# An ordering pass that counts a longer time for each transfer and lets at most eight be in flight

## The chip, the cores and the metric

The kernel runs on one core of a Trainium2 chip. The metric is the device time of one execution in microseconds (us). Three runs of the kernel before gave 2766.01, 2767.27 and 2772.61 us; the median is 2767.27 us. A profile is one more execution, recorded by the hardware profiler.

## The reference

The input x has 2048 tokens of 1024 numbers, in float32. One layer is computed:

```python
xn = rms_norm(x, mix_norm_g)
aq, ak, av, mq, mk, mv, mo, i, f, ga, gm = split(xn @ w_in)
att = chunk_band_attention(aq, ak, av, rel_bias)      # 8 heads of 64, own chunk of 64 + 8 before it
q, k = silu(causal_conv(mq, mk))                      # 4 taps
hm = rms_norm(mlstm_chunkwise(q, k, mv, i, f))        # 4 heads of 128, carried state per chunk
y = sigmoid(ga) * (att @ w_att_proj) + sigmoid(gm) * (sigmoid(mo) * hm @ w_mlstm_proj)
x = x + y @ w_out
x = x + square(relu(rms_norm(x) @ w_up)) @ w_down     # 1024 -> 4096 -> 1024
out = rms_norm(x)
```

All products must be good to float32.

## The kernel before, in words

**The work.** The tokens are cut into four blocks of 512. A product of float32 operands is made from three matmuls on rounded halves: each operand is split into a high part, rounded to the engine's fast float format, and the rest. For a weight tile ACT makes the high part (L611) and DVE the rest (L613, both in `split_now`); for an activation tile the same is done at L1321 and L1326 (`split`). The matmuls stand in `mm3` (L694 to L696) for plain products, at L779 (`quad`) and L808 (`quad_tok`) for products that are cut into seven instead of eight sub-products, with sums and differences of operands and results made by DVE (L1964 and others) and ACT (L1956 and others).

**The tiles.** On-chip tiles have fixed names and numbers of buffers: 4 `wraw` (a raw weight tile, 512 KB), 3 `wsp` (a split one), 28 `r` (split activations, 512 columns, two parts), 16 `ctx`, 6 `tmp`, 8 `bank` (PSUM). What does not fit is kept in HBM under names such as `qfar`, `kfar`, `vspill` (attention operands), `mfar`, `mvfar` (mLSTM operands), `u` (the hidden part of the feed-forward), `wsum` (differences of weight tiles). Weight loads are issued at L575, stores of all kinds at L2217 (`store`), loads of u and of mixed results at L2279 (`take_u1`), attention loads at L1350 (vspill), L1371 (kfar) and L1375 (qfar), mLSTM loads at L1715 and L1828. All of them but one small load go through the queue of the SyncE engine (SP). Transfers share eight semaphores, in turn.

At L1170 to L1175 (`norm_in`) a block of x is loaded, squared by ACT (L1172) and summed by DVE (L1175). At L1543 to L1548 (`turn`) attention probabilities are transposed by PE and split by ACT and DVE. L1512 is a matmul of scores, L1485 of probabilities with values; L1772 and L1797 are matmuls of the mLSTM part, fed by mfar and mvfar.

**The order.** It is made in two steps, both on the host, both when the program is built. First the class `Flow` runs the whole kernel as cooperating threads with estimated durations and so fixes the order in which instructions are written, and which buffer each uses. Then the class `Order` (L226) takes the finished list and orders it anew for each engine:

- `cost` and `transfer` give an estimated duration for each instruction and each transfer; `graph` finds who must wait for whom, from the regions that are read and written.
- `due` goes backwards: PE's instructions get the times at which they would run one after the other without a pause, and every other instruction the latest time at which it may start so that none of its users is late. A transfer is taken at 365 ns of SP plus `FAR`, 2500 ns, there.
- `run` (L338) goes forwards, as a simulation. It picks the engine that is free first, gives it the ripe instruction (one whose inputs are there by the estimates) with the earliest due time, PE alone the next in program order, and moves that engine's clock. A transfer costs SP 365 ns; it then passes one common queue, one after another, `REACH` (1400 ns) after the issue, for as long as `transfer` says, and has landed `LAND` (1100 ns) later. Users of what it brings become ripe on another engine only with a margin more (`MARGIN`, 2500 ns behind a transfer).
- The orders found are written into the program as fixed sequences. The pass leaves no times in it: on the chip an engine takes its instructions in that order, each as soon as its semaphores allow.

The functions that the change touches, and what calls them:

Of the kernel before, what the change touches and what calls it, by code (L numbers as in the profile page):

```python
# [96 lines left out]
class Flow:  # L97
# [77 lines left out]
    def run(self):  # L175
        while self.ready or self.blocked:
            moved = True
            while moved:
                moved = False
                for th in sorted(self.blocked, key=lambda x: (x.prio, x.n)):  # L180
                    ok, value = self._grant(th)
                    if ok:
                        self.blocked.remove(th)
                        self.now = th.at
                        self._step(th, value)
                        moved = True
            if not self.ready and not self.blocked:
                break
            if not self.ready:
                raise RuntimeError("no thread can go on")  # L190
            best = None
            for th in self.ready:
                t, frm = th.at
                for e in th.req[0].split("|"):
                    prio = th.prio
                    if e[-1] == "!":
                        e, prio = e[:-1], -1
                    start = t + self.LAT[frm].get(e, 0.0)
                    if e == "pe" and th.prio < 5:
                        start += self.SLACK  # L200
                    key = (max(self.clock[e], start), prio, th.n)
                    if best is None or key < best[0]:
                        best = (key, th, e)
            (start, _, _), th, e = best
            self.ready.remove(th)
            end = start + th.req[1]
            self.clock[e] = end
            if len(th.req) > 2:
                end += th.req[2]
            th.at = self.now = (end, e)  # L210
            self._step(th, e)
# [14 lines left out]
class Order:  # L226
# [1 line left out]

    MARGIN = dict(PE=600.0, Activation=100.0, DVE=100.0, Pool=100.0, SP=2500.0)
    WAKE = dict(PE=43.0, DVE=23.0, Activation=23.0, Pool=69.0, SP=16.0)  # L230
    REACH, LAND, FAR = 1400.0, 1100.0, 2500.0

    def __init__(self, tc):
        self.tc = tc
# [50 lines left out]
    def transfer(self, i):  # L285
        a, b = self.operands((i.outs[0], i.ins[0]))
        rows = min(list(x.ap)[0][1] for x in (a, b))
        t = self.count(a) * list(a.ap)[0][1] * 0.0099
        return max(60.0, t * (1.45 if 32 < rows <= 64 else 1.0))

    def graph(self):
# [46 lines left out]
    def run(self):  # L338
        due, n = self.due(), len(self.ins)
        at, safe, left = [0.0] * n, [0.0] * n, self.left  # L340
        clock = dict.fromkeys(self.WAKE, 0.0)
        soon = {e: [] for e in self.WAKE}
        ripe = {e: [] for e in self.WAKE}
        order = {e: [] for e in self.WAKE}
        queue = 0.0
        for k in range(n):
            if not left[k]:
                heapq.heappush(soon[self.eng[k]], (0.0, due[k], k))
        for _ in range(n):
            t, e = min((clock[e] if ripe[e] else max(clock[e], soon[e][0][0]), e)  # L350
                       for e in self.WAKE if ripe[e] or soon[e])
            while soon[e] and soon[e][0][0] <= t:
                k = heapq.heappop(soon[e])[2]
                heapq.heappush(ripe[e], (k if e == "PE" else due[k], k))
            k = heapq.heappop(ripe[e])[1]
            order[e].append(self.ins[k])
            start = max(clock[e], at[k])
            clock[e] = end = start + self.dur[k]
            if e == "SP":
                queue = max(queue, start + self.REACH) + self.transfer(self.ins[k])  # L360
                end = queue + self.LAND
            for j in self.succ[k]:
                to = self.eng[j]
                r = end + self.lag(k, j)
                at[j] = max(at[j], r)
                safe[j] = max(safe[j], r + (self.MARGIN[e] if to != "PE" and (to != e or e == "SP") else 0.0))
                left[j] -= 1
                if not left[j]:
                    heapq.heappush(soon[to], (safe[j], due[j], j))
        for o in order.values():  # L370
            for a, b in zip(o, o[1:]):
                self.tc.add_manual_dep(b, a.name, mybir.DependencyInfo(
                    mybir.DependencyClass.NoSync, mybir.DependencyReason.DATA), reason="order")
# [2337 lines left out]
```

## Time and profile before

| what | us |
|---|---|
| median of three runs | 2767.27 (2766.01 to 2772.61) |
| the profiled execution, its own time | 2769.02 |
| its span, first to last instruction | 2767.2 |
| ACT busy, DVE busy | 1493.0, 2058.8 |
| transfers by SP's queue | 676.17 MB |
| HBM read, written | 472.59 MB, 203.44 MB |

The span is what the profile's views divide up; the execution's own time has some 1.8 us around it. Engines are named PE (matmul), PEld (its weight loads, which overlap), DVE, ACT, POOL and SP; "SPq" is SP issuing a transfer. L with a number is a line of the kernel. In a list of waits a row reads "who stood idle <- who ended it: us in total, times, longest". In the chain of waits, which is followed backwards from the last instruction, a row has a start, a duration and what ran; a DMA there lasts from its issue to its landing. "r<-u" means that tile r is written from u.

### The profile page before, as it was taken

What the parts mean: (1) busy time and instruction counts of PE and PEld (TensorE: products, weight loads), DVE (VectorE), ACT (ScalarE), POOL (GpSimd) and SP (SyncE); (2) the same over time, 40 slices, a digit from 0 to 9 for tenths busy, and PEclk for the clock granted to TensorE, in tenths of its full rate; (3) what the DMA queues carried; (4) which work ended last, traced back from release to release, by engine and by line L of the source; (5) the groups of instructions that cost most, each with busy time, mean ns of one, the idle gap of its engine ahead of it and who ended that gap; (6) DMA issues with size and microseconds to landing.
All of it is one profiled execution on the core that took longest, in us unless ns stands there. A gap on an engine that the chain in (4) does not pass through costs nothing.

```text
span 2767.2 us, 38712 instructions
## 1 busy us (share of the span) xinstructions
PE 2749.7 (99%) x13054; PEld 2289.0 (83%) x13054; DVE 2058.8 (74%) x3793; ACT 1493.0 (54%) x2617; POOL 52.1 (2%) x101
## 2 busy tenths in 40 slices
PE   9999999999999999999999999999999999999999
PEld 7888888888878888888888788888888888888888
DVE  7796788767996876976667788889888656555566
ACT  5564576534454545574556566666335655554444
POOL 0010001000000000000000000000000000000000
PEclk9999999999999999999999999999999999999999
DMA  8958759759866587587888888867977667676564
GB/s 285 291 191 273 235 162 300 249 198 321 274 211 220 185 304 246 178 289 285 298 288 286 281 246 248 256 204 253 292 236 258 213 214 266 234 249 214 196 223 162
DMA packets 329190, 678.64 MB, mean 245 GB/s; under 512 B 36856, under 2 KB 67744, under 8 KB 328992
## 3 DMA queue, kind: packets, MB, share of 16 engines
q1 hardware_dynamic: 328848, 676.17, 73.6%
q8 instruction: 102, 1.67, 0.2%
q14 instruction: 96, 0.79, 0.1%
q10 hardware_dynamic: 144, 0.01, 0.0%
HBM read 472.59 MB, written 203.44 MB: 244 GB/s over the span
## 4 chain that ended last, share of the span: by engine, by line
PE 92%; DMA 3%; DVE 3%; ACT 1%; issue 1%; SPq 0%; DVEq 0%; ACTq 0%
PE bank L779 42%; PE bank L696 12%; PE bank L695 12%; PE bank L694 12%; PE bank L808 3%; PE bank L1512 2%; PE bank L1485 2%; PE bank L1543 2%; DMA r<-vspill 1%; DVE wsp L613 1%; DVE ctx L2135 1%; PE bank L1797 0%; PE bank L1798 0%; PE bank L1783 0%; PE bank L1799 0%
## 5 line engine op out<-in xcount | busy, mean ns | idle before, releaser
L779 PE MATMUL bank<-r,wsp 128*128 128x512 f32 x5544 | 1264.2, 390 | 2.4 <-ACT r L1321 1.3
L779 PEld LDWEIGHTS bank<-r,wsp 128*128 128x128 f32 x5544 | 1038.7, 188 | 220.3 <-ACT r L1321 1.7
L613 DVE TENSOR_TENSOR wsp<-wraw,wsp 128x1024 fp32r<-128x1024 f32 x458 | 559.9, 1223 | 342.9 <-ACT wsp L611 328.1
L611 ACT CAST wsp<-wraw 128x1024 fp32r<-128x1024 f32 x458 | 481.4, 1051 | 504.9 <-PE bank L695 206.1
L694 PE MATMUL bank<-r,wsp 128*128 128x512 f32 x1456 | 579.6, 398 | 2.9 <-ACT r L1321 2.7
L695 PE MATMUL bank<-r,wsp 128*128 128x512 f32 x1456 | 569.0, 391 | 0.6 <-DVE r L1326 0.6
L696 PE MATMUL bank<-r,wsp 128*128 128x512 f32 x1456 | 568.9, 391 | 0.0
L696 PEld LDWEIGHTS bank<-r,wsp 128*128 128x128 f32 x1456 | 273.4, 188 | 57.8
L694 PEld LDWEIGHTS bank<-r,wsp 128*128 128x128 f32 x1456 | 273.8, 188 | 54.8 <-ACT r L1321 3.1
L695 PEld LDWEIGHTS bank<-r,wsp 128*128 128x128 f32 x1456 | 274.1, 188 | 51.1 <-DVE r L1326 1.3
L1964 DVE TENSOR_TENSOR ctx<-bank,ctx 128x512 f32<-128x512 f32 x186 | 127.0, 687 | 100.2 <-PE bank L779 99.8
L1326 DVE TENSOR_TENSOR r<-r 128x512 fp32r<-128x512 f32 x248 | 163.6, 685 | 20.3 <-ACT r L1321 19.8
L1321 ACT CAST r<-r 128x512 fp32r<-128x512 f32 x248 | 149.0, 622 | 50.2 <-DMA r<-u 46.9
L1956 ACT COPY ctx<-bank 128x512 f32<-128x512 f32 x186 | 108.2, 582 | 84.4 <-PE bank L779 71.8
L1527 ACT ACTIVATE sc<-sc,scs 128x640 f32<-128x640 f32 (+4 forms) x128 | 97.5, 764 | 69.8 <-DVE scs L1524 64.1
L1548 DVE TENSOR_TENSOR r<-bank,r 128x512 fp32r<-128x512 f32 (+1 forms) x168 | 97.2, 596 | 20.3 <-ACT r L1546 19.3
L2295 ACT ACTIVATE ctx<-ctx 128x512 f32<-128x512 f32 x96 | 60.5, 630 | 89.6 <-DVE ctx L1964 89.5
L1518 DVE CUSTOM_DVE_ANT_0 sc<-bank,bias 128x320 f32<-128x320 f32 (+3 forms) x240 | 103.4, 462 | 3.2 <-PE bank L1512 2.4
L1546 ACT CAST r<-bank 128x512 fp32r<-128x512 f32 (+1 forms) x168 | 82.2, 518 | 43.3 <-PE bank L1543 39.2
L1485 PE MATMUL bank<-r,r 128*128 128x512 f32 x336 | 95.2, 365 | 2.2 <-DVE r L1548 2.2
L630 DVE TENSOR_TENSOR wraw<-wraw,wraw 128x1024 f32<-128x1024 f32 x76 | 92.9, 1223 | 3.0 <-DMA wraw<-in_wf 1.1
L562 DVE TENSOR_TENSOR ctx<-ctx,ctx 128x512 f32<-128x512 f32 x112 | 76.3, 687 | 24.0 <-DMA ctx<-in_wf 17.2
(269 smaller groups left out, 2748.2 us busy)
## 6 DMA issues: line engine op xcount, KB each, us to landing
wraw<-in_wf SPq DMA_DIRECT2D x178, 512.0 KB, 4.6
wraw<-wsum SPq DMA_DIRECT2D x136, 512.0 KB, 4.0
r<-u SPq DMA_DIRECT2D x224, 256.0 KB, 4.3
wraw<-in_w SPq DMA_DIRECT2D x87, 512.0 KB, 5.3
u<-ctx SPq DMA_DIRECT2D x128, 256.0 KB, 2.2
ctx<-in_wf SPq DMA_DIRECT2D x112, 256.0 KB, 4.3
wsum<-ctx SPq DMA_DIRECT2D x112, 256.0 KB, 4.2
u<-tmp SPq DMA_DIRECT2D x96, 256.0 KB, 3.4
```

Of the source, the lines that this page charges most:

```text
L611: nc.scalar.copy(w[:, 0], raw)
L613: nc.vector.tensor_sub(w[:, 1], raw, w[:, 0].bitcast(F32))
L694: mm(ps, lh, rh, start=first, stop=False)
L695: mm(ps, lh, rl, start=False, stop=False)
L696: mm(ps, ll, rh, start=False, stop=last)
L779: mm(ps, wv[:, x, k, n], a[:, y], start=new and k == 0 and x == y == 0, stop=k == 3 and x == 1, skip_group_check=True)
L1321: self.nc.scalar.copy(dst[:, 0], src)
L1326: self.nc.vector.tensor_sub(dst[:, 1], src, dst[:, 0].bitcast(F32))
L1485: nc.tensor.matmul(acc[:, :, c0:c0 + w], st, sl[:, :, o:o + w], start=n == 0, stop=n == total - 1)
L1518: nc.vector.tensor_tensor_reduce(out=e[:, x * w:x * w + w], in0=bks[x][:, :w], in1=br[:, j0 + x * w:j0 + x * w + w], op0=ALU.add, op1=ALU. ...
L1956: nc.scalar.copy(t[:, o:o + 512], ps)
L1964: nc.vector.tensor_add(t[:, o:o + 512], ps, t[:, o:o + 512])
```

## The change

Two numbers and one rule of the planner's simulation. A transfer's time in the common queue is counted at 0.0118 ns an element instead of 0.0099 (both with the same factor of 1.45 for 33 to 64 rows and the same floor of 60 ns). And a list of the last eight landing times is kept: after a transfer is begun, SP's clock in the simulation is set to no earlier than the oldest of these, so that a transfer begins only when at most seven others are in flight.

```diff
-    REACH, LAND, FAR = 1400.0, 1100.0, 2500.0
+    REACH, LAND, FAR, FLY = 1400.0, 1100.0, 2500.0, 8
...
-        t = self.count(a) * list(a.ap)[0][1] * 0.0099
+        t = self.count(a) * list(a.ap)[0][1] * 0.0118
...
-        queue = 0.0
+        queue, flying = 0.0, collections.deque([0.0] * self.FLY)
...
             if e == "SP":
                 queue = max(queue, start + self.REACH) + self.transfer(self.ins[k])
                 end = queue + self.LAND
+                flying.append(end)
+                flying.popleft()
+                clock[e] = max(clock[e], flying[0])
```

`due`, `cost`, the margins, `Flow` and the list of instructions are as before.

## The prediction, made blind

> **What bounds the kernel now.** I read the page first (busy time, DMA queues, issues).
>
> ```profile
> span 2767.2 us, 38712 instructions
> ...
> PE 2749.7 (99%) x13054; PEld 2289.0 (83%) x13054; DVE 2058.8 (74%) x3793; ACT 1493.0 (54%) x2617; POOL 52.1 (2%) x101
> ...
> q1 hardware_dynamic: 328848, 676.17, 73.6%
> ...
> r<-u SPq DMA_DIRECT2D x224, 256.0 KB, 4.3
> ```
>
> PE is busy for 2749.7 of 2767.2 us, so 17.5 us is all the time in which it does nothing. A busy PE need not be PE at its peak, so I looked at its pace in stretches of the span (columns: stretch, length, busy us and instructions of PE, PEld, DVE, ACT, POOL, granted clock, DMA share, GB/s), and in two short stretches to which I come below:
>
> ```profile
> 500.00:1100.00 600.00, 600.00 (x2651) 492.91 (x2650) 457.68 (x627) 281.98 (x414) 1.01 (x1) 1.00 0.72 245
> 85.00:115.00 30.00, 27.79 (x145) 23.73 (x144) 22.14 (x78) 15.93 (x40) 0.29 (x2) 0.94 1.02 298
> 1512.00:1546.00 34.00, 31.44 (x156) 26.30 (x154) 16.23 (x31) 11.57 (x24) 1.01 (x1) 1.00 1.01 311
> ```
>
> From 500 to 1100 us PE never idles and takes 600/2651 = 0.226 us for a matmul. That is the pace with nothing in the way; no order of transfers can better it. What the change can win is therefore idle time of PE, and nothing else. The view of waits, for PE alone, says what ended that idle time (us in total, times, longest):
>
> ```profile
> PE bank L694 <- ACT r L1321: 2.7, 1, 2.7
> PE bank L1485 <- DVE r L1548: 2.2, 1, 2.2
> PE bank L1772 <- DMA r<-mfar: 1.5, 2, 1.2
> PE bank L779 <- ACT r L1321: 1.3, 1, 1.3
> ...
> PE bank L779 <- ACT ctx L1956: 0.9, 1, 0.9
> PE bank L1797 <- DMA r<-mvfar: 0.8, 1, 0.8
> ...
> PE bank L695 <- DVE r L1326: 0.6, 2, 0.3
> ```
>
> Only two rows name a DMA. For the others the chain of waits has to be followed back. The longest stall lies near 1546 us:
>
> ```profile
> 1517.95 9.50 DMA r<-vspill
> ...
> 1527.47 0.60 SPq L1375
> ...
> 1538.13 7.33 DMA r<-u
> ...
> 1546.13 0.70 DVE r L1326
> ...
> 1546.88 0.50 PE bank L695
> ```
>
> PE waited for ACT and DVE to split a tile of u, and they waited for its load, which SP began at 1538.13 and which took 7.33 us, against a median of 4.3 us for such loads. So the 2.7 and the 0.6 just behind it (3.3 us) are a late load. The second stall, 2.2 us, is the same at one remove; the second of these rows is from the timeline of DVE, the others are from the chain:
>
> ```profile
> 100.28 8.04 DMA ctx<-in_xt
> ```
> ```profile
> 109.01 0.69 DVE L1175 TENSOR_TENSOR ctx<-ctx,ctx 128x512 f32<-128x512 f32 x1 [2.96 <-ACT ctx L1172]
> ```
> ```profile
> 109.62 0.69 DVE r L1548
> ```
>
> The load of x took 8.04 us, DVE stood idle 2.96 us at L1175 behind it, and L1548, for which PE waited, was queued behind L1175. The planner had put the sum of squares there because it believed that the load would be down by then. The other stalls hang on these loads of the chain:
>
> ```profile
> 446.86 4.26 DMA r<-mvfar
> ...
> 459.37 6.83 DMA r<-mfar
> ...
> 1206.42 4.83 DMA ctx<-x
> ```
>
> They belong to the rows of 0.8, 1.5 and 1.3 us. Together 3.3 + 2.2 + 0.8 + 1.5 + 1.3 = 9.1 us of PE's idle time have a transfer behind them, in eight events (1.1 us each). The rest of the 17.5 us is the start, the tail behind the last matmul, and waits of other kinds.
>
> **The change, part by part.** Nothing of it is an instruction. The same transfers, casts, subtractions and matmuls are issued; only the order within SP's, DVE's, ACT's and POOL's queues can differ, since PE keeps its program order in this pass. So the first term of the sum is zero.
>
> *The new limit.* SP's own timeline shows how the chip behaves at the place of the longest stall:
>
> ```profile
> 1518.68 2.65 SPq L1371 DMA_DIRECT2D r<-kfar  x4
> 1521.62 0.34 SPq L2217 DMA_DIRECT2D u<-ctx  x1
> 1522.27 0.80 SPq L575 DMA_DIRECT2D wraw<-in_wf  x1
> 1524.93 3.14 SPq L1375 DMA_DIRECT2D r<-qfar  x2
> ...
> 1535.53 0.38 SPq L1350 DMA_DIRECT2D r<-vspill  x1
> 1536.01 0.46 SPq L575 DMA_DIRECT2D wraw<-in_wf  x1
> 1536.88 1.14 SPq L1715 DMA_DIRECT2D r<-mfar  x2
> 1538.13 0.70 SPq L2279 DMA_DIRECT2D r<-u  x1
> ```
>
> The load of vspill, begun at 1517.95, lands at 1517.95 + 9.50 = 1527.45. The issue at 1527.47 is a load of qfar, which reads nothing of vspill. Behind the vspill load stand four of kfar, one store, one weight and two of qfar: it is the eighth. So the compiled program already holds SP until the transfer eight before has landed, and the new line adds no wait to the chip. It tells the planner of one that is there. Before, the planner believed that SP could begin a transfer as soon as it was ripe and the last issue was over; on the chip, what came ripe in a burst stands in SP's line, and an urgent transfer that comes ripe later stands behind it. With the limit the planner's SP wakes later, sees more ripe transfers at once and takes the most urgent by due time.
>
> For the u load of 1538.13 this is worth between 0 and 3.3 us. To save all of it, the load must be begun 2.7 + 0.2 us earlier, that is ahead of the four transfers from 1535.53 on (vspill, a weight, two of mfar). Whether its buffer was free by then the trace does not show; if not, nothing is gained there and nothing lost. I take all 3.3, because SP was held by landings in this stretch, as at 1527.47, and the four that went first are what a limit on transfers in flight would put off.
>
> *The fifth more per transfer.* A 512 KB tile is 131,072 elements, so the old count is 131,072 x 0.0099 = 1298 ns and the new one 1547 ns. The page's queue row gives 676.17 MB in 0.736 x 2767.2 us, 332 GB/s while the DMA engines work, or 1579 ns a tile; in the full stretch it is 311 GB/s, 1686 ns. The new count is 2% to 8% short, the old one 18% to 23%. Its effect is on consumers: DVE and ACT put work that waits for a load later in their queues. For the second stall it is worth between 0 and 2.2 us; I take 2.2, since the load's 8.04 us are what a planner with a full queue of slower transfers would come nearer to.
>
> The stalls of 0.8, 1.5 and 1.3 us have transfers of 4.3 to 6.8 us behind them, near the usual ones, and I leave them all. Against this, a new order draws new small stalls: bounded below by none, above by as many as now (eight); I take two at 1.1 us, 2.2 us.
>
> Sum: -3.3 - 2.2 + 2.2 = -3.3 us. On the profiled execution (2769.02 us, of which 2767.2 are the span) this is 2765.7; that execution lies 1.75 us above the median of the three shown, 2767.27, so the forecast is 2767.27 - 3.3 = **2764.0 us**. That is 0.12%; a measurement of this kernel can tell about 0.3% (8.3 us) from no change, so what I expect will hardly show.
>
> **The rivals.** *The order improves nowhere that counts.* The planner's SP may have been seldom over the limit by its own costs, or the loads that stall PE may have been unable to go earlier for want of a buffer; then stalls change places and the time stays at 2767. Against it: SP's timeline above, with eight in flight; for it: outside full stretches the DMA share is 0.72. [...]
>
> *Nearly all goes.* If both corrections reach every stall that has a transfer behind it, 9.1 us go, and with the 0.9 us of L1956 ten: 2767.27 - 9.1 = 2758.2, at best 2757.3. For it: all these stalls have the same root. Against it: in the two short stretches the DMA share is 1.02 and 1.01; there the bytes are too many for the time, and an order can only choose who is late.
>
> *Slower: the late one becomes an attention load.* That last remark also gives the other side. From 1512 to 1546 the DMA engines are full, so if u and x go first, the loads of kfar, qfar and vspill come later by what they are passed by. They feed the score matmuls of eight heads a block, which PE takes in program order and between which it has no other choice. A load that meets a full queue lands 7.33 - 4.3 = 3.0 us later than the median; each head whose loads have less than that in hand stops PE by up to 3.0 us. With four such heads in the full stretches, and the 3.3 us of the u stall saved, it is 12.0 - 3.3 = +8.7 us, 2776.0; below four it drowns in the other cases. For it: the shares of 1.02 and 1.01, and that mfar, loaded in the same way, already stops PE for 1.5 us. Against it: no row among PE's waits names kfar, qfar or vspill, so today these have time in hand.
>
> **How the numbers follow.** Forecast (some stalls go, fewer come) 0.43; improves nowhere 0.19; nearly all goes 0.15; the late attention load 0.23. The first two lie within 0.3%: 0.62. The third, as far as it goes beyond 8.3 us, is faster: 0.15. The fourth is slower: 0.23. The range runs from 2757.3, rounded to 2757, up to 2778, which is 2776.0 with two more of the 1.1 us stalls; left out are the worse half of the slow case and little else.
>
> **What would show it right or wrong.** Right: the same instruction and DMA counts; PE busy still 2750 us; no 2.7 us row with L1321 near 1546 and the u load begun ahead of vspill, weight and mfar; no idle time of 3 us on DVE at L1175; SP still held at eight. The fifth is right if ACT and DVE wait less for loads. Wrong: PE rows with L1512 or L1797 waiting for kfar, qfar, vspill or mvfar (the slow rival), or a PE busy time off 2750 us by more than 2 us, since then something other than stalls has changed. A time above 2776 or below 2757 refutes the forecast.

## The result, and the profile after

| | before | after |
|---|---|---|
| median of 11 runs, us | 2769.07 (2766.01 to 2772.96) | 2761.15 (2759.37 to 2762.92) |
| profiled execution, us | 2769.02 | 2762.92 |
| its span, us | 2767.2 | 2761.1 |

The ratio is 0.997, with a 95% interval of 0.9961 to 0.9979: 7.9 us less by the medians, 6.1 us by the two profiled executions. The change helps, by about as much as a measurement of this kernel can tell. From here on L numbers of the kernel after are 3 higher than those of before, because the change added three lines ahead of them, and those of the experiments 27 higher.

The page first, two lines of it:

```profile
span 2761.1 us, 38681 instructions
...
PE 2748.6 (100%) x13054; PEld 2291.3 (83%) x13054; DVE 2060.5 (75%) x3793; ACT 1490.9 (54%) x2617; POOL 49.9 (2%) x101
```

The counts of engine instructions are those of before; the totals differ by semaphore instructions only. PE's idle time is 2761.1 - 2748.6 = 12.5 us instead of 17.5 us: 5.0 of the 6.1 us. What ended it, in the view of waits for PE alone:

```profile
PE bank L782 <- ACT r L1324: 2.0, 1, 2.0
PE bank L782 <- ACT ctx L1959: 2.0, 1, 2.0
PE bank L782 <- ACT r L1326: 1.1, 1, 1.1
PE bank L438 <- DVE ones L435: 1.0, 1, 1.0
PE bank L1645 <- DVE cum L1641: 0.7, 2, 0.3
PE bank L697 <- ACT ctx L1779: 0.5, 1, 0.5
PE bank L782 <- DVE r L1329: 0.2, 1, 0.2
```

The rows of before that had a transfer behind them (2.7 + 0.6, 2.2, 1.5, 0.8 us) are gone. The fifth, the 1.3 us behind a load of x near 1212 us, has become 2.0 us, the first row. The second row was 0.9 us before and the sixth 0.2; the third is new. In the two short stretches, of which the first lost 2.2 us of PE before and the second 2.6, PE now never stops, and the DMA share in the second is as full as it was:

```profile
85.00:115.00 30.00, 30.00 (x164) 25.63 (x163) 24.75 (x85) 17.97 (x44) 0.58 (x4) 1.00 0.99 266
1512.00:1546.00 34.00, 34.00 (x170) 28.92 (x169) 20.66 (x50) 15.10 (x31) 1.01 (x1) 1.00 1.05 315
```

SP's timeline shows why. The first load of u is begun at 1525.28, 12.9 us earlier than before (11.5 us measured from the same matmul, since PE is 1.4 us ahead by then), and three more follow it, all ahead of mfar and vspill:

```profile
1525.28 0.33 SPq L2282 DMA_DIRECT2D r<-u  x1
1526.33 0.34 SPq L578 DMA_DIRECT2D wraw<-in_wf  x1
1527.18 2.50 SPq L2282 DMA_DIRECT2D r<-u  x3
1529.84 0.32 SPq L2220 DMA_DIRECT2D u<-ctx  x1
1530.24 0.40 SPq L1718 DMA_DIRECT2D r<-mfar  x1
...
1533.10 1.14 SPq L1353 DMA_DIRECT2D r<-vspill  x2
```

And near 109 us DVE's sum of squares (L1178) no longer waits. It is the last of seven sums, which are made one after another. Before, it had stood 2.96 us, to 109.01; now it comes at 115.04, behind the work that PE waits for (L1551, at 106.96):

```profile
115.04 0.69 DVE L1178 TENSOR_TENSOR ctx<-ctx,ctx 128x512 f32<-128x512 f32 x1
```

Its load is begun no earlier than before (at 102.20, where it had been 100.28). The stall went because DVE does the sum later.

Of the larger stalls, the first hangs on a load of x, which took 6.12 us here and 4.83 before; the second and the third end with ACT:

```profile
1207.72 6.12 DMA ctx<-x
```

The second row ends with ACT (L1959) emptying a bank at 1148.21 to 1148.69, after a run of DVE and ACT work in which no transfer shows.

### The profile page after: what moved, and what is told of

Its sections match the earlier page's. It is cut to its first block, busy times and chain, and to the rows that moved or that the text cites. A ratio compares the mean times of both kernels' runs of the same rounds, so it can differ in the third digit from the quotient of the medians.

```text
span 2761.1 us, 38681 instructions
## 1 busy us (share of the span) xinstructions
PE 2748.6 (100%) x13054; PEld 2291.3 (83%) x13054; DVE 2060.5 (75%) x3793; ACT 1490.9 (54%) x2617; POOL 49.9 (2%) x101
## 4 chain that ended last, share of the span: by engine, by line
PE 95%; DVE 2%; ACT 1%; issue 1%; DMA 0%; SPq 0%; DVEq 0%; ACTq 0%
PE bank L782 42%; PE bank L697 13%; PE bank L699 13%; PE bank L698 13%; PE bank L811 3%; PE bank L1515 2%; PE bank L1488 2%; PE bank L1546 2%; PE bank L1802 1%; PE bank L1801 1%; DVE ctx L2138 1%; PE bank L1800 1%; PE bank L1786 0%; DVE wsp L616 0%; PE bank L862 0%
## 5 line engine op out<-in xcount | busy, mean ns | idle before, releaser
L782 PE MATMUL bank<-r,wsp 128*128 128x512 f32 x5544 | 1266.6, 391 | 5.4 <-ACT r L1324 2.0
L782 PEld LDWEIGHTS bank<-r,wsp 128*128 128x128 f32 x5544 | 1040.5, 188 | 223.7 <-ACT r L1324 2.5
L1959 ACT COPY ctx<-bank 128x512 f32<-128x512 f32 x186 | 107.9, 581 | 81.8 <-PE bank L782 70.1
L1551 DVE TENSOR_TENSOR r<-bank,r 128x512 fp32r<-128x512 f32 (+1 forms) x168 | 97.2, 597 | 20.1 <-ACT r L1549 19.1
L1515 PE MATMUL bank<-r,r 128*128 128x320 f32 (+3 forms) x480 | 85.7, 305 | 0.0
```

The lines of the kernel that those rows point to most:

```text
L782: mm(ps, wv[:, x, k, n], a[:, y], start=new and k == 0 and x == y == 0, stop=k == 3 and x == 1, skip_group_check=True)
L1515: nc.tensor.matmul(bks[x][:, :w], q[:, y, i * P:(i + 1) * P], kf[:, f * P + x * w:f * P + x * w + w], start=y == 0, stop=y == 1)
L1959: nc.scalar.copy(t[:, o:o + 512], ps)
```

## The experiments

For these the pass was rewritten so that one function `plan` takes the count a transfer is charged (`rate`), the limit (0 for none), a fixed order for some engine, and stretches of the planner's own clock in which the full change's numbers hold. `plan(0.0099, 0)` gives the orders of before, `plan(0.0118, 8)` those of after. An engine with a fixed order takes its next instruction when its inputs are there; all others are planned around it. Each experiment is one expression in place of `plan(0.0118, 8)`. Each time stands against runs of the kernel before on the same chip, whose medians were 2768.0 to 2769.3 us.

Theory A, with which I began, is the prediction's in a simpler form: each half of the change cures its own stall through the order of the transfers (the prediction had the count act through the queues of DVE and ACT). Theory B says that the gain is in PE's own order. I had to add it, because my prediction was wrong on a point of the code: PE does not keep its program order in this pass. It takes the lowest of those that are *ripe*, so it can step over a matmul whose operands the planner believes to be late, and 373 of its 12,738 places differ between before and after. Theory C is luck: a new order, other stalls.

### One half alone: the limit

```diff
-order = self.plan(0.0118, 8)
+order = self.plan(0.0099, 8)
```

> The old count of 0.0099 with the limit of eight. Times against the kernel before (2769). Theory A (each half of the change wins its own stalls, through the order of the transfers): the long stall of PE near 1546 us goes (2.7 + 0.6 us) and the 2.2 us near 109 us, which a longer count was to cure, stays: -3 to -4 us, near 2765.5. Theory B (the gain is in PE's own order, which this pass also makes): 103 of PE's places differ from before against 373 in the full change, so about a quarter of 8 us: -2 us, 2767. Theory C (any new order falls within a few us of the old by luck): anything from 2764 to 2774, with stalls at new places.

Measured: 2771.15 us, ratio 1.0009 (1.0000 to 1.0018). The largest of PE's waits:

```profile
PE bank L1539 <- DVE scs L1545: 4.2, 2, 3.3
PE bank L1799 <- DMA r<-mfar: 3.4, 2, 2.8
PE bank L1512 <- DVE r L1575: 2.4, 2, 1.7
```

The 2.4 us holds the stall near 110 us. The 3.3 us is a stall of the score matmuls near 1548 us, and it is one that I had not thought of. SP begins the first load of u at 1531.52, 6.6 us earlier than before; but ACT and DVE, planned for faster transfers, are sent to split u earlier still. The waits of all engines from 1535 to 1552 us, and one row of DVE's timeline:

```profile
ACT r L1348 <- DMA r<-u: 5.9, 3, 3.0
DVE r L1353 <- ACT r L1348: 4.5, 3, 2.4
```
```profile
1544.67 0.69 DVE L1353 TENSOR_TENSOR r<-r 128x512 fp32r<-128x512 f32 x1 [2.45 <-ACT r L1348]
```

Behind these splits, in DVE's queue, stands the work on the scores that PE waits for. The load came sooner, and the two engines stood before it all the same. The 2.8 us behind mfar, near 457 us, were 1.2 before. Theory A fails in its first half.

### The other half alone: the count

```diff
-order = self.plan(0.0118, 8)
+order = self.plan(0.0118, 0)
```

> The new count of 0.0118 without the limit. Theory A: the 2.2 us stall near 109 us and the ones of 0.8 and 1.5 us behind mvfar and mfar go, the one near 1546 us stays at least in part: -3 to -5 us, 2764 to 2766. Theory B: 512 of PE's places differ from before, more than in the full change, so the whole gain or more: 2760 to 2762. Theory C: 2764 to 2774.

Measured: 2767.05 us, ratio 0.9995 (0.9986 to 1.0004). PE's waits begin:

```profile
PE bank L806 <- ACT ctx L1983: 2.0, 1, 2.0
PE bank L806 <- ACT r L1350: 1.0, 1, 1.0
PE bank L462 <- DVE ones L459: 1.0, 1, 1.0
PE bank L721 <- DMA ctx<-xn: 0.9, 1, 0.9
PE bank L1570 <- DVE sc L1558: 0.9, 2, 0.5
```

The stall near 110 us is gone, and those near 1546 us have shrunk from 3.3 to 1.6 us (0.9 in the last row, 0.7 in one not shown), so the count alone does about half of what I had given to the limit. But the new stalls of the full change near 720 and 1150 us are there too, some 2.0 us are still lost near 460, and the sum is no gain that can be told from none. The two halves do not add: +0.1% and no difference alone, -0.3% together.

### PE's order alone, and the rest without it

```diff
-order = self.plan(0.0118, 8)
+order = {**self.plan(0.0099, 0), "PE": self.plan(0.0118, 8)["PE"]}
```

> PE's order from the full change, the orders of SP, DVE, ACT and POOL from before. Theory A (transfers): the late loads are as late as before, so the stalls stay: 0 to -2 us, 2767 to 2769. Theory B (PE's order): PE meets other matmuls while a load is late, so most of the gain is there: -6 to -8 us, 2761 to 2763.

Measured: 2776.28 us, ratio 1.0026 (1.0016 to 1.0036).

```diff
-order = self.plan(0.0118, 8)
+order = self.plan(0.0118, 8, fixed={"PE": self.plan(0.0099, 0)["PE"]})
```

> PE held to its order from before, the other engines planned anew with the full change's costs and limit. Theory A: nearly the full gain, -6 to -8 us, 2761 to 2763. Theory B: at most -2 us, or slower, 2767 or more. If both give half, the two orders each carry a part.

Measured: 2781.91 us, ratio 1.0048 (1.0035 to 1.0061). Theory B falls by the first of these: PE's new order alone costs 7.7 us. But Theory A had the second one at a full gain, and it costs 13 us:

```profile
PE bank L806 <- ACT r L1348: 5.0, 1, 5.0
PE bank L1247 <- POOL r_far L1279: 4.8, 1, 4.8
```

The second row tells the reason: a transpose that PE's old order has at that place waits for POOL, whose work the new plan puts later (489.81 before, 495.43 in the full change, 497.62 here). A half of one plan and a half of another stop each other.

### SP's order alone, and the rest without it

Theory A', after these: the late loads decide, and SP's order says which are late. Theory D: what counts is that the planner's times, for all engines, are near the chip's.

```diff
-order = self.plan(0.0118, 8)
+order = self.plan(0.0099, 0, fixed={"SP": self.plan(0.0118, 8)["SP"]})
```

> SP held to its order from the full change; PE, DVE, ACT and POOL planned anew around it with the old count and no limit. Theory A' (the late loads decide, and SP's order says which are late): at least half of the 8 us, 2765 or less, and no stall of over 1 us near 109 and 1546 us. Theory D (the orders are one plan, and what counts is that the planner's times for all engines are near the chip's): the other engines still believe in fast transfers, so little or no gain, 2766 to 2772.

Measured: 2763.73 us, ratio 0.9982 (0.9973 to 0.9991), 5.6 us of the 7.9. PE's largest wait that is not the start:

```profile
PE bank L1570 <- DVE sc L1558: 1.3, 1, 1.3
```

The first load of u is begun at 1521.93, as long before the same matmul as in the full change (14.8 us), and only 0.4 us of stall is left near 1548 us. But the 1.3 us stand at 111.6, where Theory A' had nothing over 1 us: just ahead DVE stands 1.26 us at the sum of squares that comes at 115.04 in the full change, although SP's order is the same in both.

```profile
109.86 0.69 DVE L1202 TENSOR_TENSOR ctx<-ctx,ctx 128x512 f32<-128x512 f32 x1 [1.26 <-ACT ctx L1199]
```

```diff
-order = self.plan(0.0118, 8)
+order = self.plan(0.0118, 8, fixed={"SP": self.plan(0.0099, 0)["SP"]})
```

> SP held to its order from before; the other engines planned anew around it with the new count and the limit. Theory A': the u load near 1546 us is as late as before, so at best the 2.2 us near 109 us go: 2766 to 2769. Theory D: the planner knows when the loads really land, though they land late, and lets PE, DVE and ACT work around them: half of the gain or more, 2765 or less.

Measured: 2815.54 us, ratio 1.0171 (1.0157 to 1.0185). PE's longest waits stand in one row, and the chain ahead of the longest names the late one, a weight load that SP began only behind a row of stores:

```profile
PE bank L806 <- ACT wsp L638: 19.8, 8, 9.7
```
```profile
1298.85 6.07 DMA wraw<-in_wf
```

I had not expected it to be this dear; neither theory did, and both miss here. By the first of the pair Theory A' holds for the time and for the stall near 1546 us, and D, which had little or no gain, falls there: the other engines still counted with 0.0099. Near 109 us it is the other way about, since with one and the same order of SP the stall depends on the count by which DVE was planned. Neither theory is enough alone.

### One place alone

```diff
-order = self.plan(0.0118, 8)
+order = self.plan(0.0099, 0, span=((1400e3, 1560e3),))
```

> The plan from before, but the new count and the limit hold for transfers that the planner begins between 1400 and 1560 us of its own clock, which is some 1430 to 1595 us of the trace; 47 of PE's places and 88 of SP's differ from before. If the stall near 1546 us is cured where it stands: -3.3 us (2.7 + 0.6) to -4.1 us (what PE gained there in the full change by its position in the order), near 2765, and the rest of the trace as before. If the cure needs the changes of order before it: 0 us, 2769.

Measured: 2764.36 us, ratio 0.9982 (0.9974 to 0.9991), -5.0 us. PE's waits:

```profile
PE bank L1512 <- DVE r L1575: 2.2, 1, 2.2
PE bank L806 <- ACT r L1348: 1.0, 1, 1.0
PE bank L462 <- DVE ones L459: 1.0, 1, 1.0
PE bank L806 <- ACT ctx L1983: 0.9, 1, 0.9
```

The 2.2 us near 109 stay to a tenth, the 2.7 + 0.6 near 1546 are gone. So the stall is cured where it stands. The rows of mfar and mvfar near 466 and 450 us (1.2 and 0.8 us before) are missing here too, although nothing ahead of 1400 us was re-planned; stalls that hang on how long a transfer takes come and go between programs whose orders are the same up to there, by 2 us in this pair. The profiled execution, 2761.47, is also the second fastest of its eleven (2761.2 to 2767.15).

### Both ends, without the middle

```diff
-order = self.plan(0.0118, 8)
+order = self.plan(0.0099, 0, span=((0.0, 600e3), (1280e3, 4000e3)))
```

> The new count and the limit up to 600 and from 1280 us of the planner's clock, the old ones between. In the full change PE gained 6.7 us by the first and 4.1 to 4.7 us by the last stretch, and lost 5.3 us between (new stalls near 718, 1148 and 1215 us and a half clock behind the second). If the stretches are independent: 2769 - 11 = 2758, faster than the full change by some 3 to 5 us. If each new plan draws its own stalls anew: 2760 to 2766.

Measured: 2757.49 us (2757.01 to 2757.62), ratio 0.9961 (0.9948 to 0.9975), -11.8 us by the medians and -10.8 by the ratio, as forecast from independent stretches.

```profile
PE bank L806 <- ACT r L1348: 1.2, 1, 1.2
PE bank L462 <- DVE ones L459: 1.0, 1, 1.0
PE bank L806 <- ACT ctx L1983: 0.9, 1, 0.9
PE bank L1669 <- DVE cum L1665: 0.6, 2, 0.3
```

The stalls of the middle are back at their old 1.3 and 0.9 us (here 1.2 and 0.9), the one near 718 is gone, and the cures at both ends hold.

### Controls: less, more, fewer

A sixth less, without a limit: `self.plan(0.0083, 0)`.

> A control in the wrong direction: transfers counted at 0.0083, a sixth less than before, no limit; 529 of SP's places differ from before. If what counts is how near the planner's times are to the chip's: no stall of before goes and some grow, 2769 to 2776. If any new order is as likely to be better as worse (luck): 2762 to 2776, with the stalls near 109 and 1546 us gone as often as not.

Measured: 2797.6 us, ratio 1.0104 (1.0091 to 1.0118), 30 us slower and beyond both forecasts. The largest row names a load openly:

```profile
PE bank L1799 <- DMA r<-mfar: 9.4, 2, 5.5
PE bank L721 <- ACT r L1348: 3.2, 1, 3.2
PE bank L1512 <- DVE r L1575: 3.1, 3, 1.7
```

The rate of the full stretch: `self.plan(0.0129, 8)`.

> 0.0129 (the 311 GB/s of the full stretch) with the limit of eight. If nearness to the chip's times counts: as good as the full change or better, 2757 to 2762, with the stretches near 109 and 1546 us free of stalls; over-counted elsewhere, so it may lose some in the half-empty stretches near 718 and 1150 us. If luck: 2757 to 2772.

Measured: 2768.72 us, ratio 0.9999 (0.9990 to 1.0008). The stretch near 1546 us is clean, but there are three waits of 0.4 to 1.3 us near 155 us and one of 1.1 us at 450, and near 720 and 1155 us PE loses 1.0 and 2.0 us, much as in the full change. Nearer to the full stretch's rate was not better.

Half the limit: `self.plan(0.0118, 4)`.

> 0.0118 with a limit of four, half of what the chip has; 1396 of SP's places differ from before. If the gain is in SP choosing later and so by urgency, four serve as well as eight: 2758 to 2763. If it is in the planner being near the chip, four are too few, loads that could run ahead are held back in the order, and part of the gain is lost: 2763 to 2772.

Measured: 2758.46 us (2757.25 to 2759.36), ratio 0.9961 (0.9948 to 0.9975).

```profile
PE bank L806 <- ACT ctx L1983: 2.0, 1, 2.0
PE bank L462 <- DVE ones L459: 1.0, 1, 1.0
PE bank L1669 <- DVE cum L1665: 0.7, 2, 0.3
```

Four are not the eight at which SP is held (before, it began a transfer at 1527.47, when the one eight earlier had landed at 1527.45), and they serve at least as well: the only stall above 1 us besides the start is the one near 1148. The first load of u is begun at 1520.78, which by PE's progress is the place it has in the full change.

The full change once more, on the chip of these four:

> The orders of the full change once more, on the chip of these runs, made by the rewritten pass: 2761 against 2769, a ratio of 0.996 to 0.998. It tells how far a ratio moves between chips, and whether the two-ended plan, at 0.9961, beats it.

Measured: 2760.33 us (2759.06 to 2762.45), ratio 0.9967 (0.9956 to 0.9979). It repeats the stalls of the kernel after near 718 and 1149 us (1.1 and 2.0 us), but not the 2.0 us near 1213: the load of x took 4.22 us instead of 6.12 there, and 0.2 us is left. So the size of that row depends on the execution and not on the order alone. The limit of four is 1.9 us below this run on the same chip, the two-ended plan 2.8 us below it on another chip; the intervals of the ratios overlap, so that either is better than the change is likely and not shown.

## Why the prediction was right, and where it was not

The sign, the range (2757 to 2778) and the kind of the effect were right: no instruction more or less, PE's pace untouched, the gain in idle time of PE that has a transfer behind it. The forecast of -3.3 us was less than half of the -7.9. The range is wide enough to hold the kernel before as well (2769.07), so a time inside it proves little. And the 2764.0 lies nearer to the measured 2761.15 than -3.3 does to -7.9 by luck: it was counted from the median of three runs, 1.8 us below that of eleven.

*Which stalls go.* I took the 3.3 and the 2.2 us as won, and both went. I left the stalls of 0.8, 1.5 and 1.3 us in place; the first two went in the full change's trace, but also in the trace of the experiment that re-planned only the place near 1546 us, so their 2.3 us cannot be put down to the change for sure. Two new stalls of 1.1 us were charged; what came was 1.1 us near 718, 1.1 us more near 1148, 0.7 us more near 1213 (not in the second execution) and 0.3 us more near 445, in sum 3.2 us. That term was too small by about half, and the right size would have made the forecast worse. Won 5.5 and 2.3, lost 3.2: this is 4.6 of the 5.0 us of idle time. PE's busy time is 1.1 us less as well, for which no run shows a cause. The last 1.8 us lie between the profiled executions and the medians: the profiled one of the kernel after is the slowest of its eleven (2762.92).

*What I had left out: the clock behind a stall.* Stretches on both sides of the stall near 109 us, before the change, and behind the one near 1148 us after it (the column behind POOL is the granted clock):

```profile
105.00:111.00 6.00, 3.79 (x23) 3.11 (x23) 3.04 (x5) 1.76 (x4) 0.00 (x0) 1.00 1.07 251
111.00:115.00 4.00, 4.00 (x17) 3.58 (x16) 3.21 (x18) 1.96 (x7) 0.00 (x0) 0.57 1.07 332
```
```profile
1150.00:1154.00 4.00, 4.00 (x12) 3.17 (x11) 1.52 (x4) 1.86 (x3) 0.00 (x0) 0.57 0.83 239
```

A share of 0.57 over 4 us, with half speed as the only other grant in the trace, is 3.4 us at half speed (0.50 from 111.22 to 114.63), which by my estimate is 1.7 us of PE's work, beside the 2.2 us. In the kernel after, one matmul of L782 follows another every 0.43 us in the stretch behind the stall near 1148, and every 0.23 us from 1153.6 on. So the stall near 109 cost 3.9 us, and the new one near 1148 cost its 2.0 and 1.7 more. Between the two kernels this cancels, so it is not why -3.3 was too small; but my own row for 85 to 115 us showed a granted clock of 0.94, and I still took idle time of PE for all that an order can win. In the two-ended plan the stall near 109 is gone and the one near 1148 lasts 0.9 us, and no such stretch is left but the last microseconds of the run (a granted clock of 1.000 over its span, 0.999 after): an estimated 1.7 us of its lead over the kernel after. Length alone does not decide: the 2.2 us near 109 and the 2.0 us near 1148 had such a stretch behind them, and the 2.7 us near 1546, before, had none (a granted clock of 1.00 from 1536 to 1552).

The traces tell these stalls apart. In each trace the half-speed stretches start whole multiples of 3.4133 us apart (before: at 111.22 and, in the last microseconds, at 2766.79, which is 778 of them later; after: at 1150.15 and, just behind the span, at 2761.24, 472 of them later), and all but those at the end are 3.413 us long or a multiple. On this grid the 2.2 us near 109 lie in one interval, and the stalls near 1546 are cut in two, with 1.4 and 1.6 us of idle PE:

```profile
107.80:111.22 3.42, 1.21 (x7) 0.86 (x7) 2.21 (x5) 1.76 (x4) 0.00 (x0) 1.00 1.08 247
1541.40:1544.82 3.42, 2.04 (x12) 1.54 (x10) 0.32 (x1) 0.00 (x0) 0.00 (x0) 1.00 1.03 389
1544.82:1548.23 3.41, 1.85 (x7) 1.32 (x8) 2.10 (x8) 2.19 (x3) 0.00 (x0) 1.00 1.05 403
```

Over all fourteen traces, up to the last microseconds, every grid interval in which PE stood for 1.96 us or more was followed by one at half speed (22 of 22, with 2.21 us before and 1.99 us after among them); of those with 0.9 to 1.9 us, 5 of 50 were.

*The step on the limit* was wrong as put. I had it cure the u load by itself, and the count cure the load of x. Measured by how long before one and the same score matmul (the 7181st of PE's, at 1541.4 us before) the first u load is begun, it was 3.3 us before, 9.9 with the limit alone, 4.3 with the count alone, and 14.8 in the full change, with SP's new order alone, with the limit of four, with the count of 0.0129 and with the plan changed at that place only. The limit moves the load, as I said, but 9.9 us were not enough for an ACT and a DVE planned with the old count; the 14.8 of SP's new order were, with 0.4 us of stall left. The count moves the load by little, and with 4.3 us leaves 1.6 us of stall. With both there is no stall, not even in the second execution of the full change, where the load was begun only 10.6 us ahead. That 14.8 us is the same in five kernels suggests that there the load waits for its buffer and no order can begin it sooner; this is argued, not shown. The eight that I counted on SP's timeline are there, and they do not matter as a number, since four served as well.

*The step on the count* held as put, that DVE and ACT do the work on a load later. ACT's wait for loads of u, over the whole span, follows the count by which ACT was planned, and not the order of SP: with 0.0099 it is 46.9 us before, 50.2 with the limit alone and 49.7 with SP's new order; with 0.0118 it is 20.0 us in the full change, 25.2 with the count alone and 26.0 with SP's old order. The controls lie on both sides, at 62.1 with 0.0083 and 17.5 with 0.0129. This is the sign that the prediction named for the count.

*PE keeps its program order in this pass* was false, and with it the slow rival's remark that PE has no other choice. The runs show that PE's order belongs to the plan: alone it costs 7.7 us, and kept from before it costs 13.

*The rivals.* The slow one, attention loads that come late in the full stretch, did not happen: with the DMA share at 1.05, no row names kfar, qfar or vspill. An order can only choose who is late, and here the passed-over had time in hand, as the row against it said. The rival that nearly all goes (2758.2) was near for those stalls and wrong for the net, by the new ones. Counting less than before is not the way either: it cost 30 us.

## What to carry to other kernels

Where one engine is busy 99% of the time, list its stalls one by one and follow each to the transfer behind it: the sum of those, with the half-speed time behind them, is about what a new order can win (9.1 and 1.7 us here; the plan of both ends won 10.8 by the ratio, 11.8 by the medians), and a planner that believes transfers to be faster than they are can lose nearly four times as much (30 us against 7.9). Let the planner choose transfers late, by a limit on what is in flight, and charge them about what the queue moved while it worked (0.0118 ns for four bytes is 339 GB/s, the run's own rate 332); the 311 GB/s of the full stretch gave no gain. Then check stretch by stretch, since a better plan in two places drew new stalls in a third, and keeping the old one there seems worth another half of the gain. A plan is one piece: PE's order from the new plan with the rest from the old one cost 8 us, and the old order of PE or of SP, with the rest planned anew around it, 13 and 46 us. Only SP's new order, with the rest planned around it, kept most of the gain.

## What the runs showed of the hardware that I had not expected

A stall of PE of 2.0 to 2.2 us that lay in one interval of a 3.4133 us grid was followed by 3.4 us at half speed, which nearly doubles its price, and one of 2.7 us that the grid cut in two went without. In the control with 0.0083, whose granted clock was 0.996 over 2795.2 us, such stretches add up to 20.5 us, by my estimate 10 of its 30 us. And two programs with one order up to 1400 us had two stalls of 1.2 and 0.8 us behind loads in one execution and neither in the other; the full change, run twice, loaded one tile of x in 6.12 and in 4.22 us, and stood 2.0 and 0.2 us for it.
